# An encoder trunk on one core: where the first modulation products run, how the squares of y are added, and where the last SSD group's items stand

## The chip, the cores and the metric

One core of a Trainium2 chip runs the whole program in one launch. The metric is device microseconds of one execution, given as the median of several runs. Engines are named as the profile names them: PE is TensorE's matmul and PEld its weight load, DVE is VectorE, ACT is ScalarE, POOL is GpSimd and SP is SyncE, which here only issues DMAs.

## The reference, cut to what matters

```python
cond = jax.nn.silu(c)                                  # c: (1, 1024)
for i in range(2):
    mod = cond @ mod_w[i] + mod_b[i]                   # (1, 3072)
    shift, scale, gate = jnp.split(mod, 3, axis=-1)
    hn = rms_norm(x, norm_w[i]) * (1.0 + scale[:, None, :]) + shift[:, None, :]
    y = dilated_attention_mixer(hn, ...) if i == 0 else bi_ssd_mixer(hn, ...)
    x = x + gate[:, None, :] * y                       # x: (1, 1024, 1024)
return rms_norm(x, final_norm_w)

def bi_ssd_mixer(h, ...):                              # its end
    y = y_f + y_b + xs * d_skip[:, None]               # 8 groups of 256 channels
    y = y.reshape(b, s, 2048) * jax.nn.silu(z)
    return rms_norm(y, norm_w) @ w_out
```

## The kernel before, in words

All tensors are held with channels on the 128 partitions and the 1024 tokens along the free axis, so x is eight tiles of 128x1024. The order of work is written out by hand: every engine runs its own instructions in the order in which the program emits them, and waits only for data and for buffers. A dense float32 product is made of three passes, high by high, high by low and low by high, of operands split in two parts: ACT writes the high part (L271 for weights, L293 for the normalised input), DVE the low part (L272, L294). The three matmuls are L376 to L378, and L1004 to L1006 in the output projections. The tile `big` (128x1024) has 27 buffers, and the weight staging tile `wraw` has 4.

**The start (`layer0`).** SP issues the eight tiles of x, then the weights of the modulation in blocks of 128x1024 (`mod_load`, L158). Block 2j is the shift and block 2j+1 the scale of channel tile j; a block holds eight 128x128 pieces, one for each tile of c, and its result is a column of 128 numbers. ACT squares x (L851), PE sums the squares over the partitions with a matrix of ones (L856), and from the sums comes the reciprocal root r: ACT gives a first value (L898, L901), and one Newton step on DVE (L913, L914) mends it, for both halves of the tokens. For a block, `mods` multiplies the weights by the numbers of cond: on POOL (L173, one instruction over the whole block, then two additions, L177) or on ACT (L169, eight instructions). For the blocks that ACT multiplied, and for block 0 and 1, `half` adds the pieces up on DVE (L867, two additions). `fin(j)` lets PE sum what is left over the partitions, two matmuls of one column to a block (L197), and DVE adds the bias (L201) and makes the factor gs (L204). Then `prep(j)` normalises tile j in two halves: DVE L287, ACT L293 (high), DVE L294 (low). The loop over kt (eight turns) runs 18 matmuls of 512 columns to a turn; in it stand `fin(kt + 1)`, `prep(kt + 1)`, the split of the weights of turn kt + 2, the products of blocks 2kt+6 (ACT) and 2kt+7 (POOL), and one `half`. The tables of the rotary angles are made on the side: 44 small instructions on DVE before the loop, the last 14 on POOL, emitted in turn 5.

**The end of layer 1 (`out1`, `first`).** The last SSD group, group 7, runs beside the end of its own dense products and beside the first 14 steps of the output projection; a step is one kt with four matmul groups, 12 matmuls. `weave` spreads the group's items (from `ssd_items`) over this main list by one weight each; `balance`, used for the groups before it, spreads by two estimates of an item, its time on PE and on DVE. The items are A1 (transposes), A2 (the chunk states: L1424 and L1425, then L1434 and L1435), B1 (L1449 and L1455 on DVE, exponentials on ACT), M (L1471, L1473, L1476 on DVE) and B2 (the output matmuls L1487, then L1491 on DVE and a product with z on POOL, L1495). One empty item stands ahead of B1(7). For the projection, `fetch` loads a half tile of y, and `prep(r, kt)` makes its squares (L1554 on POOL for kt under 3, L1556 on ACT), lets POOL add them to a sum (L1558), and splits y times the norm weight: ACT L1561, DVE L1562. The low part is put off to the start of the next step, where DVE runs it in order. Steps use the split y of kt, and `prep` runs up to three steps ahead. The root mean square of y is needed only after the projection (`total`, one matmul with ones).

Of the kernel before, what the change touches and what calls it, by code (L numbers as in the profile page):

```python
# [15 lines left out]
OP = mybir.AluOpType  # L16
# [75 lines left out]
class Trunk:  # L92
# [96 lines left out]

    def mod_fin(self, i, b, *accs):  # L190

        nc = self.nc
        p = self.bank("a2", [P, H2])
        for k, acc in enumerate(accs):
            n = acc.shape[1]
            for c in range(0, n, P):
                nc.tensor.matmul(p[:, k * P:k * P + 1], acc[:, c:c + P], self.ones[:, :1], start=c == 0, stop=c + P == n)  # L197
        m = self.modv[i]
        for k in range(len(accs)):
            c = slice(b + k, b + k + 1)  # L200
            nc.vector.tensor_add(m[:, c], p[:, k * P:k * P + 1], self.vec[:, 16 + 24 * i + b + k:17 + 24 * i + b + k])  # L201
            if b + k < 16 and (b + k) % 2:
                d = (b + k) // 2
                nc.vector.scalar_tensor_tensor(self.gs[i][:, d:d + 1], m[:, c], 1.0,  # L204
                                               self.vec[:, 64 + 8 * i + d:65 + 8 * i + d], op0=OP.add, op1=OP.mult)
# [607 lines left out]
    def layer0(self):  # L813
# [33 lines left out]
        self.w_dma(3)  # L847

# [19 lines left out]

        def fin(j):
            self.mod_fin(0, 2 * j, *[mw.pop(2 * j + s)[:, :2 * P] for s in range(2)])  # L870
# [28 lines left out]
        for h in range(2):  # L899
# [3 lines left out]
            half(h)  # L903
        self.w_split(0)
        mods(2, nc.scalar)
        mods(3, nc.gpsimd)
        def prep(kt):
            if kt < KT:
                for h in range(2):
                    self.hn_tile(0, kt, h * H2, H2, xt[kt][:, h * H2:h * H2 + H2], r[h], self.hn)  # L910
# [4 lines left out]
        fin(0)  # L915
        prep(0)
        self.w_split(1)
        mods(4, nc.scalar)
        mods(5, nc.gpsimd)
        self.finish()  # L920
        self.flush()
        half(2)
        half(4)
        accs = [[self.acc() for _ in range(2)] for _ in range(2)] + [[self.bank("a0", [P, H2], 2) for _ in range(2)]]
        evac = self.evac0 = self.attn_evac(0)
        for kt in range(KT):
            load(kt + 4)
            if 3 < kt + 4 < KT:
                self.w_dma(kt + 4)
            if kt + 3 < KT:  # L930
                mods(2 * kt + 6, nc.scalar)
                mods(2 * kt + 7, nc.gpsimd)
            for m in range(3):
# [6 lines left out]
                elif m == kt == 0:  # L940
                    fin(1)
# [856 lines left out]
```

## Time and profile before

| | us |
|---|---|
| median of 3 runs (1858.36 to 1860.43) | 1859.21 |
| the profiled execution | 1857.47 |
| its span, first to last instruction | 1855.5 |
| PE busy in the span | 1777.3 |
| DVE busy in the span | 1420.6 |
| ACT busy in the span | 956.6 |
| POOL busy in the span | 328.0 |

The page gives busy time and share of each engine, then the span in 40 equal slices with a digit for the busy tenths. A timeline row is start, duration, engine, line, operation, what it writes and reads with shapes, and in brackets the idle time before it and what ended it; a row marked x8 merges eight instructions. PE is busy nearly everywhere, so what can be gained lies where it is not: the first 90 us, and the stretch around the end of the last SSD group, from about 1595 to 1697 us.

### The profile page before, as it was taken

To read this page: it belongs to the slowest core of one execution; us is meant where nothing else is said; L and a number is where in the kernel's file an instruction comes from. 1 tells how busy PE (TensorE), PEld (TensorE's weight loads), DVE (VectorE), ACT (ScalarE), POOL (GpSimd) and SP (SyncE) were. 2 spreads that over 40 slices of the span, in tenths; PEclk is the share of its full clock that TensorE was granted. 3 is DMA by queue.
4 is the path that set the end of the run, shared out by engine and by line. 5 is a ranking of instruction groups with operands and counts; after the bars stand their busy time and mean duration, and the time that the engine had idled before them with its cause. 6 is when DMAs were issued, how large, how long until landed. Compare 5 with 4: busy or idle time off the path is not lost.

```text
span 1855.5 us, 28487 instructions
## 1 busy us (share of the span) xinstructions
PE 1777.3 (96%) x10050; PEld 1453.4 (78%) x10050; DVE 1420.6 (77%) x3219; ACT 956.6 (52%) x2095; POOL 328.0 (18%) x493
## 2 busy tenths in 40 slices
PE   5899999999999999999999999999999999798997
PEld 2678788878788888788878788888888878676787
DVE  7966578766755655666687989899898989897975
ACT  5454445544444544544435656565656565565632
POOL 4611112112211221010110101010101010233310
PEclk7899999999999999999999999999999999999998
DMA  6242234322412131173313243433323342344542
GB/s 249 94 122 90 84 103 129 99 84 87 120 47 58 56 80 55 59 229 136 100 41 97 69 118 82 114 89 93 100 83 108 80 111 78 114 133 140 187 160 96
DMA packets 99733, 193.65 MB, mean 104 GB/s; under 512 B 15624, under 2 KB 23048, under 8 KB 99592
## 3 DMA queue, kind: packets, MB, share of 16 engines
q1 hardware_dynamic: 86600, 167.32, 29.7%
q0 software_dynamic: 12288, 23.86, 4.7%
q8 instruction: 79, 1.29, 0.3%
q10 hardware_dynamic: 704, 0.66, 0.1%
q14 instruction: 62, 0.51, 0.1%
HBM read 169.00 MB, written 16.48 MB: 100 GB/s over the span
## 4 chain that ended last, share of the span: by engine, by line
PE 72%; DVE 17%; ACT 4%; issue 3%; DMA 3%; SPq 0%; ACTq 0%; DVEq 0%; POOL 0%
PE acc L376 16%; PE acc L378 15%; PE acc L377 15%; PE a L1487 3%; PE a L1425 2%; DVE wlo L272 2%; PE a L719 2%; PE a L1004 2%; PE a L1005 2%; PE a L1006 2%; DVE big L1336 2%; PE a L704 2%; PE acc L1006 2%; PE acc L1004 2%; PE acc L1005 2%
## 5 line engine op out<-in xcount | busy, mean ns | idle before, releaser
L376 PE MATMUL acc<-big,whi 128*128 128x512 f32 (+1 forms) x1520 | 631.2, 415 | 13.0 <-ACT big L293 12.4
L377 PE MATMUL acc<-big,whi 128*128 128x512 f32 (+1 forms) x1520 | 595.3, 392 | 2.7 <-DVE big L294 2.6
L378 PE MATMUL acc<-big,wlo 128*128 128x512 f32 (+1 forms) x1520 | 595.3, 392 | 0.3 <-DVE wlo L272 0.3
L376 PEld LDWEIGHTS acc<-big,whi 128*128 128x128 f32 x1520 | 288.0, 189 | 78.6 <-issue 15.8
L378 PEld LDWEIGHTS acc<-big,wlo 128*128 128x128 f32 x1520 | 287.5, 189 | 64.3 <-DVE wlo L272 1.2
L377 PEld LDWEIGHTS acc<-big,whi 128*128 128x128 f32 x1520 | 288.7, 190 | 53.0 <-DVE big L294 6.1
L272 DVE TENSOR_TENSOR wlo<-wraw,whi 128x512 fp32r<-128x512 f32 (+1 forms) x297 | 214.1, 726 | 83.1 <-ACT whi L271 80.1
L271 ACT CAST whi<-wraw 128x512 fp32r<-128x512 f32 (+1 forms) x302 | 181.3, 612 | 85.5 <-PE a L1005 27.3
L695 ACT ACTIVATE sm<-sm,nb 128x256 f32<-128x256 f32 (+1 forms) x192 | 89.3, 466 | 194.9 <-DVE nb L693 192.2
L1336 DVE SCALAR_TENSOR_TENSOR big<-acc,cv,big 128x512 f32<-128x512 f32 (+1 forms) x248 | 169.2, 741 | 6.5 <-ACT big L1328 6.5
L1495 POOL TENSOR_TENSOR big<-big,yt 128x128 f32<-128x128 f32 x128 | 65.3, 531 | 586.7 <-DVE yt L1491 586.6
L1457 ACT ACTIVATE E<-E,nacb 128x128 f32<-128x128 f32 x256 | 81.8, 391 | 143.1 <-DVE E L1449 129.4
L706 DVE COPY pt<-a 128x512 f32<-128x512 f32 (+1 forms) x96 | 57.6, 600 | 73.2 <-PE a L704 73.1
L690 DVE CUSTOM_DVE_ANT_0 sm<-a,cst 128x256 f32<-128x256 f32 (+1 forms) x192 | 64.9, 375 | 60.3 <-PE a L685 60.0
L1004 PE MATMUL a<-big,whi 128*128 128x256 f32 (+1 forms) x304 | 99.2, 326 | 0.0
L1006 PE MATMUL a<-big,wlo 128*128 128x256 f32 (+1 forms) x304 | 98.2, 323 | 0.1
L1005 PE MATMUL a<-big,whi 128*128 128x256 f32 (+1 forms) x304 | 97.9, 322 | 0.0
L1005 PE MATMUL acc<-big,whi 128*128 128x512 f32 x224 | 88.9, 397 | 5.9 <-DVE big L1562 3.1
L592 POOL DMA_DIRECT2D rt<-kT x92 | 50.3, 561 | 243.0 <-ACT kT L532 145.8
L1006 PE MATMUL acc<-big,wlo 128*128 128x512 f32 x224 | 89.5, 399 | 3.2 <-DVE wlo L272 2.4
L1004 PE MATMUL acc<-big,whi 128*128 128x512 f32 x224 | 90.5, 404 | 0.0
L1328 ACT ACTIVATE big<-acc,cv 128x512 f32<-128x512 f32 x62 | 44.5, 770 | 86.4 <-PE acc L378 76.0
(254 smaller groups left out, 3181.7 us busy)
## 6 DMA issues: line engine op xcount, KB each, us to landing
wraw<-in_win SPq DMA_DIRECT2D x186, 256.0 KB
acs<-acsd SPq DMA_DIRECT2D x64, 512.0 KB
wraw<-in_wout SPq DMA_DIRECT2D x112, 256.0 KB
big<-in_modw SPq DMA_DIRECT2D x48, 512.0 KB
yd<-big POOLq DMA_DIRECT2D x14, 512.0 KB, 4.4
big<-yd SPq DMA_DIRECT2D x28, 256.0 KB
vT<-mix POOLq DMA_DIRECT2D x20, 256.0 KB, 4.2
big<-in_xT SPq DMA_DIRECT2D x8, 512.0 KB
```

The lines of the kernel that those rows point to most:

```text
L271: self.nc.scalar.copy(dst_hi, src)
L272: self.late.append((lambda: self.lo_engine.tensor_sub(dst_lo, src, dst_hi.bitcast(F32)), tile))
L376: mm(o, hi[:, cols], x_[:, t0:t0 + n], start=first, stop=False, **kw)
L377: mm(o, hi[:, cols], x_[:, H2 + t0:H2 + t0 + n], start=False, stop=False, **kw)
L378: mm(o, lo[:, cols], x_[:, t0:t0 + n], start=False, stop=last, **kw)
L695: nc.scalar.activation(sm[:, h, :W], sm[:, h, :W], AF.Exp, bias=nb[:, h:h + 1], scale=0.125, accum_out=stat[:, h, 1, i:i + 1])
L1004: mm(o, hi[:, c], x[:, t:t + n], start=kt == 0 and (n == H2 or m % 2 == 0), stop=False, **kw)
L1005: mm(o, hi[:, c], x[:, H2 + t:H2 + t + n], start=False, stop=False, **kw)
L1006: mm(o, lo[:, c], x[:, t:t + n], start=False, stop=kt == nkt - 1, **kw)
L1336: nc.vector.scalar_tensor_tensor(y[:, lo:hi], a[:, lo + o:hi + o], w[:, cv, k:k + 1], y[:, lo:hi], op0=OP.mult, op1=OP.add)
L1457: nc.scalar.activation(E[:, h], E[:, h], AF.Exp, bias=self.nacb[:, c, 4 * g + h:4 * g + h + 1])
L1495: nc.gpsimd.tensor_mul(z, z, t[:, r])
```

## The change

In the start, the products of blocks 1, 2, 3, 4, 6, 10 and 14 are made by PE itself: eight matmuls of one column on the raw weights, with a column of cond as the moving operand. Block 0 is multiplied by DVE, the other eight (5, 7, 8, 9, 11, 12, 13, 15) by ACT, and these nine go through `half`. POOL multiplies none. Weight blocks 8 to 11 are asked for ahead of the first wait of SP, and 12 to 15 in the first two turns. The Newton step runs for the first half of the tokens, then `fin(0)` and `prep` of that half, and then for the second. `fin(1)` is put ahead of the loop.

In `out1`, for the first half of the tokens, y is fetched in pairs of tiles, its squares are all made by ACT and written in pairs into a tile of their own; POOL adds seven such tiles into the first, three of them inside the 14 steps and four behind them, and PE sums both halves of the tile (two matmuls for one). `balance` takes the place of `weave`, the empty item has 6.0 us of DVE time to its name, and the fetches of the first y tiles stand some items ahead of their `prep`.

```diff
-    def mod_fin(self, i, b, *accs):
...
         self.w_dma(3)
+        load(4)
+        load(5)
...
+        pe, act = (1, 2, 3, 4, 6, 10, 14), (5, 7, 8, 9, 11, 12, 13, 15)
+
         def fin(j):
-            self.mod_fin(0, 2 * j, *[mw.pop(2 * j + s)[:, :2 * P] for s in range(2)])
+            p = self.bank("a0", [P, 2, P], 2) if j < 2 else self.bank("a2" if j % 2 else "a3", [P, 2, P])
+            for k in (1, 0):
+                w = mw.pop(2 * j + k)
+                n = KT if 2 * j + k in pe else 2
+                for c in range(n):
+                    x = self.cond[:, c:c + 1] if n == KT else self.ones[:, :1]
+                    nc.tensor.matmul(p[:, k, :1], w[:, c * P:c * P + P], x, start=c == 0, stop=c == n - 1)
+            m = self.modv[0]
+            c = slice(2 * j, 2 * j + 2)
+            nc.vector.tensor_add(m[:, c], p[:, :, 0], self.vec[:, 16 + 2 * j:18 + 2 * j])
+            nc.vector.scalar_tensor_tensor(self.gs[0][:, j:j + 1], m[:, 2 * j + 1:2 * j + 2], 1.0,
+                                           self.vec[:, 64 + j:65 + j], op0=OP.add, op1=OP.mult)
...
-        mods(0, nc.gpsimd, 1)
-        mods(1, nc.gpsimd, 1)
         for h in range(2):
             merge(6, slice(h * H2, h * H2 + H2))
             total(sq[6], False, True, (h,))
+        mods(0, nc.vector, 1)
+        half(0)
...
             nc.scalar.activation(u[h], r[h], AF.Square)
-            half(h)
         self.w_split(0)
-        mods(2, nc.scalar)
-        mods(3, nc.gpsimd)
...
             nc.vector.scalar_tensor_tensor(r[h], u[h], 1.5, r[h], op0=OP.add, op1=OP.mult)
-        fin(0)
-        prep(0)
+            if h == 0:
+                fin(0)
+            prep(0, (h,))
         self.w_split(1)
-        mods(4, nc.scalar)
-        mods(5, nc.gpsimd)
+        mods(5, nc.scalar)
         self.finish()
         self.flush()
-        half(2)
-        half(4)
+        fin(1)
...
         for kt in range(KT):
-            load(kt + 4)
+            if kt < 2:
+                load(kt + 6)
...
-            if kt + 3 < KT:
-                mods(2 * kt + 6, nc.scalar)
-                mods(2 * kt + 7, nc.gpsimd)
...
             self.w_split(kt + 2)
+            for b in (2 * kt + 6, 2 * kt + 7):
+                if b in act:
+                    mods(b, nc.scalar)
             self.finish()
             self.flush()
-            if kt + 3 < KT:
-                half(2 * kt + 6)
+            for b in (2 * kt + 4, 2 * kt + 5):
+                if b in act:
+                    half(b)
...
         if g == 7:
-            items.append((1500, lambda: None, 0, 0))
+            items.append((1500, lambda: None, 0, 6.0))
...
+        def add_pair(k):
+            for n in range(2):
+                c = slice(n * H2, n * H2 + H2)
+                nc.gpsimd.tensor_add(pairs[0][:, c], pairs[0][:, c], pairs[k][:, c])
+            pairs[k] = None
...
-            if r == 0 and kt < 3:
-                nc.gpsimd.tensor_mul(sq, y, y)
-            else:
-                nc.scalar.activation(sq, y, AF.Square)
-            if kt:
+            if r == 0:
+                if kt % 2 == 0:
+                    pairs.append(self.big())
+                    if kt in (8, 10, 12):
+                        add_pair(kt // 2 - 3)
+                sq = pairs[-1][:, kt % 2 * H2:kt % 2 * H2 + H2]
...
+            nc.scalar.activation(sq, y, AF.Square)
+            if kt and r:
                 nc.gpsimd.tensor_add(ys[r]["sq"][:, :H2], ys[r]["sq"][:, :H2], sq)
...
         def first(ps):
             m = tail[0][:]
-            for i in range(4):
-                m.insert(len(m) - 10 + 2 * i, (1, lambda i=i: prep(0, i)))
-            weave(m + [(2600, f) for _, f in ps[0][:14]], tail[1])
+            for at, f, k in ((1, prep, 3), (2, prep, 2), (3, fetch, 4), (4, prep, 1), (6, prep, 0), (8, fetch, 2), (12, fetch, 0)):
+                m.insert(len(m) - at, (1, lambda f=f, k=k: f(0, k), 0, 0.7 if f is prep else 0))
+            balance(m + [(2600, f, 2.76, 1.4) for _, f in ps[0][:14]], tail[1])
+            add_pair(4)
+            add_pair(5)
...
                 prep(0, kt)
+            add_pair(6)
...
+            add_pair(7)
```

## Rows read from the trace of the kernel before

**Rows 1.** The page: busy time, share of the span, instructions.

```profile
PE 1777.3 (96%) x10050; PEld 1453.4 (78%) x10050; DVE 1420.6 (77%) x3219; ACT 956.6 (52%) x2095; POOL 328.0 (18%) x493
```

**Rows 2.** Stretches of the start: window and length, busy of each engine, granted clock, DMA.

```profile
7.30:20.30 13.00, 12.93 (x24) 5.42 (x24) 9.20 (x36) 9.27 (x10) 3.26 (x2) 1.00 1.02 411
20.30:37.30 17.00, 1.97 (x8) 1.85 (x8) 16.71 (x15) 6.45 (x16) 15.24 (x10) 0.56 0.41 158
37.30:93.50 56.20, 49.80 (x200) 38.48 (x201) 50.67 (x74) 30.75 (x76) 30.61 (x27) 0.83 0.34 118
```

**Rows 3.** Timeline of PE, 37 to 94 us.

```profile
39.28 0.79 PE L378 MATMUL acc<-big,wlo 128*128 128x512 f32 x1 [0.34 <-DVE wlo L272]
...
41.16 1.70 PE L197 MATMUL a<-ones,big 128*128 128x1 f32 x8
...
58.27 0.80 PE L377 MATMUL acc<-big,whi 128*128 128x512 f32 x1 [1.72 <-DVE big L294]
...
69.88 0.94 PE L197 MATMUL a<-ones,big 128*128 128x1 f32 x8
...
89.48 0.39 PE L376 MATMUL acc<-big,whi 128*128 128x512 f32 x1
...
93.33 0.39 PE L378 MATMUL a<-big,wlo 128*128 128x512 f32 x1
```

**Rows 4.** Timeline of DVE, 20 to 90 us.

```profile
20.85 3.29 DVE L867 TENSOR_TENSOR big<-big 128x512 f32<-128x512 f32 x2
...
26.61 2.38 DVE L913 SCALAR_TENSOR_TENSOR big<-big,sm 128x512 f32<-128x512 f32 x1
...
65.67 1.14 DVE L867 TENSOR_TENSOR big<-big 128x512 f32<-128x512 f32 x2
...
74.66 1.82 DVE L867 TENSOR_TENSOR big<-big 128x512 f32<-128x512 f32 x2
...
86.94 1.41 DVE L287 SCALAR_TENSOR_TENSOR kT<-big,gs,pt 128x512 f32<-128x512 f32 x2
88.48 1.41 DVE L294 SCALAR_TENSOR_TENSOR big<-kT,modv,big 128x512 fp32r<-128x512 f32 x2
```

**Rows 5.** Timeline of POOL: the first products, first and last of the angle tables.

```profile
17.04 6.82 POOL L173 TENSOR_TENSOR big<-big,cond 128x1024 f32<-128x1024 f32 x3 [16.08 <-DMA big<-in_modw]
...
71.28 2.04 POOL L481 TENSOR_TENSOR vT<-vT,vT 128x192 f32<-128x192 f32 x2
...
83.15 0.83 POOL L498 TENSOR_TENSOR V<-vT,vT 128x192 f32<-128x192 f32 x1
```

**Rows 6.** ACT's groups, 20 to 93.5 us: count, busy, mean ns, idle before.

```profile
L169 ACT ACTIVATE big<-big,cond 128x128 f32<-128x128 f32 x56 | 17.0, 388 | 0.0
```

**Rows 7.** Stretches of the late part, columns as in Rows 2.

```profile
1595.40:1628.80 33.40, 28.27 (x128) 21.94 (x126) 24.54 (x45) 12.55 (x31) 9.78 (x10) 0.95 0.47 134
1628.80:1641.50 12.70, 12.70 (x71) 10.48 (x69) 9.16 (x18) 11.16 (x26) 3.53 (x2) 1.00 0.49 160
1641.50:1696.50 55.00, 44.30 (x291) 32.94 (x290) 54.76 (x106) 37.03 (x86) 22.99 (x22) 0.97 0.44 126
```

**Rows 8.** DVE's groups, 1595.4 to 1628.8 us, columns as in Rows 6.

```profile
L1562 DVE SCALAR_TENSOR_TENSOR big<-big,sv,big 128x512 fp32r<-128x512 f32 x4 | 3.1, 776 | 7.4 <-ACT big L1561 7.4
...
L272 DVE TENSOR_TENSOR wlo<-wraw,whi 128x512 fp32r<-128x512 f32 x4 | 2.7, 684 | 0.7 <-ACT whi L271 0.7
```

**Rows 9.** Timeline of DVE at the first projection steps.

```profile
1631.92 0.42 DVE L1455 TENSOR_TENSOR cb<-a,cst 128x256 f32<-128x256 f32 x1 [2.99 <-PE a L1452]
...
1644.35 1.76 DVE L1562 SCALAR_TENSOR_TENSOR big<-big,sv,big 128x512 fp32r<-128x512 f32 x1
```

**Rows 10.** DVE's groups, 1628.8 to 1697.5 us.

```profile
L1562 DVE SCALAR_TENSOR_TENSOR big<-big,sv,big 128x512 fp32r<-128x512 f32 x10 | 11.2, 1115 | 0.0
```

**Rows 11.** POOL's groups, 1628.8 to 1697.5 us.

```profile
L1558 POOL TENSOR_TENSOR big<-big,big 128x512 f32<-128x512 f32 x10 | 16.6, 1659 | 41.0 <-ACT big L1556 41.0
L1495 POOL TENSOR_TENSOR big<-big,yt 128x128 f32<-128x128 f32 x15 | 11.3, 773 | 11.7 <-DVE yt L1491 11.6
```

More of the change, by code (lines that the diff above doesn't have):

```diff
@@ L188, in mod_acc @@
             nc.vector.tensor_add(out, acc, odd)
-    def mod_fin(self, i, b, *accs):
[L192 to L205, printed above, removed]
     def mod_sum(self, i, b, accs):
@@ L902, in layer0, with prep @@
             nc.scalar.activation(u[h], r[h], AF.Square)
-            half(h)
         self.w_split(0)
-        mods(2, nc.scalar)
-        mods(3, nc.gpsimd)
-        def prep(kt):
+        def prep(kt, hs=range(2)):
             if kt < KT:
-                for h in range(2):
+                for h in hs:
                     self.hn_tile(0, kt, h * H2, H2, xt[kt][:, h * H2:h * H2 + H2], r[h], self.hn)
@@ L1530, in out1 @@
         nc, io = self.nc, self.io
-        xin, x2, cut, ybuf = {}, {}, {}, {}
+        xin, x2, cut, ybuf, pairs = {}, {}, {}, {}, []
         ys, st = [{} for _ in range(2)], [{} for _ in range(2)]
@@ L1536, in fetch @@
                 return
-            buf = ybuf[r, kt] = self.big()
-            if kt < 14:
-                nc.sync.dma_start(buf[:, :H2], self.yd[kt][:, H2 * r:H2 * r + H2])
+            if r:
+                buf = self.big()
+                ybuf[r, kt] = buf, buf[:, :H2]
+                if kt < 14:
+                    nc.sync.dma_start(buf[:, :H2], self.yd[kt][:, H2:])
+            elif kt < 14:
+                buf = self.big()
+                for k in range(2):
+                    y = buf[:, H2 * k:H2 * k + H2]
+                    ybuf[r, kt - kt % 2 + k] = buf, y
+                    nc.sync.dma_start(y, self.yd[kt - kt % 2 + k][:, :H2])
+            else:
+                ybuf[r, kt] = None, None
+        def add_pair(k):
[3 more added lines that the diff above has]
+            pairs[k] = None
         def prep(r, kt):
@@ L1545, in prep @@
             fetch(r, kt)
[L1546 to L1547 removed]
+            buf, y = ybuf.pop((r, kt))
             if kt >= 14:
                 y = self.ylast[kt - 14][:, H2 * r:H2 * r + H2]
[L1550 removed]
+            if r == 0:
[4 more added lines that the diff above has]
+                sq = pairs[-1][:, kt % 2 * H2:kt % 2 * H2 + H2]
+            elif kt == 0:
                 ys[r]["sq"] = self.big()
                 sq = ys[r]["sq"][:, :H2]
[L1553 to L1557 removed]
+            else:
+                sq = buf[:, H2:]
+            nc.scalar.activation(sq, y, AF.Square)
+            if kt and r:
                 nc.gpsimd.tensor_add(ys[r]["sq"][:, :H2], ys[r]["sq"][:, :H2], sq)
@@ L1615, in total @@
             def total():
-                ys[r]["s"] = self.all_sum(ys[r], 0, H2, self.acc())
+                if r:
+                    ys[r]["s"] = self.all_sum(ys[r], 0, H2, self.acc())
+                    return
+                p = ys[r]["s"] = self.acc()
+                for n in range(2):
+                    nc.tensor.matmul(p, self.ones, pairs[0][:, n * H2:n * H2 + H2], start=n == 0, stop=n == 1)
             def start():
                 ys[r]["v"] = self.rstd_start(ys[r]["s"], 2 * D, H2)
-            return [(0.5, out), (1, total), (1, start)]
+            return [(0.5, out)] + [(2, lambda: None)] * (r == 0) + [(1, total), (1, start)]
         def first(ps):
             m = tail[0][:]
-            for i in range(4):
-                m.insert(len(m) - 10 + 2 * i, (1, lambda i=i: prep(0, i)))
-            weave(m + [(2600, f) for _, f in ps[0][:14]], tail[1])
+            for at, f, k in ((1, prep, 3), (2, prep, 2), (3, fetch, 4), (4, prep, 1), (6, prep, 0), (8, fetch, 2), (12, fetch, 0)):
[3 more added lines that the diff above has]
+            add_pair(5)
             for _, f in ps[1][:2]:
```

5 lines of the change are left out of this document (removed).

## The prediction

> **What bounds the kernel now.** I read the page first: PE is busy 96% of the span [rows 1], so a change can give back only what PE loses, some 78 us, and the question is where it loses it. The windows tell: most of it lies at the two places that the diff touches. At the start, PE ends the sums of squares at 20.3, and until 37.3 it is busy for 1.97 us of 17, while DVE is busy for 16.71 of 17 and POOL for 15.24 [rows 2]. The first matmul that needs a low part of the weights runs at 39.28, and the last of the eight turns is issued at 93.33 [rows 3]. In the loop DVE is busy for 50.67 of 56.2 us, POOL for 30.61, and the mean granted clock of PE is 0.83 [rows 2]: PE waits for DVE, and falls to 1.2 GHz after waits, such as the 1.72 us ahead of 58.27 [rows 3].
>
> The DVE timeline says why DVE takes so long. The two additions of one `half` take 1.14 us at 65.67, but 3.29 at 20.85, where POOL runs its 128x1024 products of 2.3 us each; one 512-wide step of Newton takes 2.38 [rows 4, 5], while other two-operand instructions of that width take 0.70 (half of 1.41) [rows 4]. DVE is slowed by POOL's work beside it.
>
> The late windows show a second place. From 1595.4 to 1628.8 PE is idle for 5.1 of 33.4 us [rows 7]; in it DVE stands 7.4 us at L1562, the low part of y, waiting for ACT, which itself waited for y to be loaded [rows 8]. From 1641.5 to 1696.5 DVE is busy for 54.76 of 55 us and PE for 44.30 [rows 7]: DVE is the bound. There too it is slowed: L1562 means 1115 ns where POOL adds squares, against 776 before [rows 8, 10].
>
> **The change part by part: up to the first matmul.** I work out the quiet time of what DVE does from 20.3 to 37.3. Two scalings of the sums (0.7 each), two `half` (1.14 each), four Newton steps and two L287 (0.70 each), and the small additions with gs (0.4) come to 8.3 us, so 8.4 of the 16.7 are POOL's doing. The change takes POOL's products out; one `half` goes (block 1 is PE's), and the other, with a product of 1.2 us for block 0, goes into the time before 20.3, where DVE is busy for only 9.20 of 13 us [rows 2]; block 0 arrived by 17.04 [rows 5], so some 0.4 us of it may stick out past 20.3, which I take into the range. That leaves 16.7 - 8.4 - 2.3 = 6.0 us.
>
> But one thing comes with it. The last 14 instructions of the angle tables stand on POOL behind all products, from 71.28 to 83.98, 12.7 us [rows 5]. Nothing is ahead of them now, and what they read is done on DVE before 17 us, so they run from about 17 to 30, under this very chain. Their price is read where they ran before: a `half` beside them took 1.82 against 1.14 at 74.66 [rows 4], the worst of the pairs there; I take a third on the mean, 2.0 us, with nothing and a doubling (6.0) as ends. The doubling is what POOL's large products did. The chain then takes 8.0 to 8.4 instead of 17.0: **8.6 us earlier** (4.6 to 10.6), the first full matmul group near 30.7. The weights are there: blocks 0 to 7 come by the same queue as before, 8 to 11 behind them, where the DMAs stood idle (0.41 of the stretch used [rows 2]). `fin(1)` stands ahead of the loop in PE's queue, 16 matmuls; 4 take 0.94 us [rows 3], so 3.8, or 6.8 at the low clock (1.70 for 4 [rows 3]). PE is free from 20.3 and does ten for `fin(0)` first, so it ends by 30, in time.
>
> **The loop.** It took 93.7 - 39.3 = 54.4 us. After the change the turns hang on one ring: `fin` on PE, then DVE's addition and gs (0.3), L287 (1.41), L294 (1.41), the low part of the weights (0.5, three quarters of the 0.68 of 512 columns [rows 8]), then the `half`s of the blocks that ACT multiplied, and these are what the next `fin` waits for. That is 3.6 us of DVE for each of six turns and seven `half`s at 1.14, 29.6 in all. ACT keeps up: a block costs it 8 x 0.3 = 2.4 us [rows 6], in the worst turn two, beside 1.9 of its own work. `fin` is dearer on PE: 10 matmuls (2.4 us) where one block is raw, 4 (0.95) for blocks 8, 9 and 12, 13; six of them cost 4 x 2.4 + 2 x 0.95 = 11.5. With some 6.5 us for the first turn, which starts at the low clock, and 4.1 for the last (89.48 to 93.33, and one issue [rows 3]): 6.5 + 29.6 + 11.5 + 4.1 = 51.7. PE's own work in a turn, 4.1 + 2.4, is under the ring's 7.3, so the ring sets it, and PE waits 0.6 to 1.6 us in each turn. I add 1.7 us for falls of the clock after such waits, since it fell after 1.72 at 58.27: 53.4, **1.0 us gained** (2.7 to minus 8). So the ring takes back most of what the quiet DVE gives: the added PE work is not hidden, as it stands between two DVE stages of the same turn.
>
> **The last SSD group.** The items' order I worked out from their weights. In the dense part the A items come about one dense step earlier, the first y tiles are fetched seven items before the end and split only two items before it, so DVE no longer stands at L1562 for a load. PE's 5.1 us idle there should go: **5 us** (1 to 6.5; some falls to A2's own chain). Then `balance` puts B1(7) behind the third projection step instead of the first: two steps of 12 matmuls at 0.227 us, 5.4 us later on PE, which cancels the 5. So the first L1455 of DVE, at 1631.92, which waits for that matmul [rows 9], comes at about the same time, and from there DVE is the bound. What it has left is less: the low parts for two more steps are behind it (0.74 + 0.68 each, 2.8 us), and of the additions of squares on POOL six instead of ten [rows 11] fall into this stretch. Each costs DVE about a microsecond: L1562 took 1.76 at 1644.35 [rows 9], 0.98 over the quiet 776 [rows 8], so 4.0. Products with z on POOL stay. Against it, at the end the last two chunks stand together behind the last step, and DVE waits for ACT's exponentials: 1.5 us, bounded by 0 and 4 (no row shows this order). Net 2.8 + 4.0 - 1.5 = 5.3. The second matmul of `total` is a plain float32 one of 512 columns; 24 instructions made 12 of these in 12.93 us [rows 2], so 1.1 us more, in a part where PE is the bound. The eight additions that POOL makes behind the steps fall where DVE has room, and cost nothing; without this room, up to 8 us of DVE. **4.2 us gained** (9 to minus 2).
>
> **The sum.** 8.6 + 1.0 + 4.2 = 13.8 us. The profiled execution took 1857.47, so 1843.7 on its scale; the median of the runs is 1.7 above it, and from 1859.21 comes **1845.4 us**.
>
> **Rivals.** (1) The angle tables on POOL hold DVE as much as its products did: the chain doubles, 4.0 us of the gain go, 1849.4. For: each of their instructions reads SBUF. Against: 1.82 and not 3.29 for a `half` [rows 4]. The Trainium skill's page SBUF - State Buffer, section "Who interferes with whom", says that a DVE instruction with two SBUF inputs is blocked for the whole of a GpSimd instruction that reads SBUF, if that came first; by it the tables can cost DVE at most their own length, and the 1.82 agrees.
>
> (2) The late part gives nothing: the chunks that come later, and the wait at the end, take all of it. 1859.2 - 9.6 = 1849.6. For: DVE has no idle time there [rows 7], so order alone can't help. Against: six additions for ten.
>
> (3) Both parts give their upper ends: 10.6 + 2.7 + 7.5, 1838.4. For: both upper ends need only quiet on DVE.
>
> (4) Runs of one-column matmuls let the clock fall. In the four turns with ten, `fin` takes 4.25 instead of 2.35 (by 1.70 against 0.94 [rows 3]), and about a third of the wide matmuls' time is lost, 3 us a turn, 12 in all: 1857.4, no difference. For: the turns with waits show 0.83. Against: at 69.88 four of them run at 0.94, at full clock.
>
> (5) Slower: PE stays at 1.2 GHz through the whole loop, since a turn now has 2.4 us of one-column work and a wait in it. All its work takes 1.8 times as long (1.70 over 0.94): eight turns of 4.1 and 11.5 of `fin` make 80 us instead of 53.4. From 30.7 the loop ends at 110.7, 17 later than before, 12.8 later with the late part's gain: 1872. It decides once PE's work in a turn, 1.8 x 6.5 = 11.7, is over the ring's 7.3 in most turns. Against: before, the clock came back within each turn (0.83 as a mean).
>
> **How the numbers follow.** Forecast 0.45, (1) 0.13, (2) 0.12, (3) 0.13, (4) 0.12, (5) 0.05. A change under 0.2%, 3.7 us, is about what a measurement can't tell from none; the border is 1855.5. Faster: the forecast, (1), (2), (3) and a third of (4), 0.87; same: the rest of (4), 0.08; slower 0.05. The range goes from (3) with 1.4 of the unknown costs below it, 1837, to just short of (4), 1856.
>
> **What would show it.** First L378 of the loop near 30 to 31 and the last near 84; no L173 on POOL, and the angle tables on it at 17 to 30; PE's waits in the loop ended by L867 or gs, not by L293. Late: DVE's wait at L1562 gone, L1455 of B1(7) near 1631.9 less the 9.6 gained ahead of it, six L1558-like additions in the steps, B2(0) some 5 us earlier than the start's gain alone would put it. Wrong if the loop's clock lies under 0.75, if the first L378 comes after 35, or if DVE's busy share in the steps stays at 0.99 for as long as 65 us.

## The result and the profile after

The changed kernel takes **1840.92 us** (median; 1839.99 to 1841.28), the kernel before 1859.82 beside it: a ratio of 0.9896 (95% interval 0.9878 to 0.9913), 18.9 us faster. Beside the experiments below the kernel before had medians of 1856.76 to 1857.84, so a fair figure is 16 to 19 us. Its profiled execution has a span of 1839.0 us against 1855.5, 16.5 less, and it is these 16.5 that the traces can place. Lines of the changed kernel differ in number: mm3's three matmuls, before L376 to L378, are L359 to L361; `fin`'s matmuls are L866, `half` is L852, Newton L912 and L913, `prep` L270, L276, L277, the low parts of weights L255; late, the pair additions are L1554, the low part of y L1582, B1 L1450, M L1469, B2 L1485, the steps L1002 to L1004.

| place | before, us | after, us | gained so far | here |
|---|---|---|---|---|
| first full group of the loop (first matmul on a low part) | 39.28 | 29.87 | 9.4 | +9.4 |
| PE leaves the loop (first matmul behind its last turn) | 93.56 | 86.49 | 7.1 | -2.3 |
| fourth of ACT's table loads behind 70 us | 158.24 | 147.16 | 11.1 | +4.0 |
| an ACT table load as the dense part with the last group begins | 1591.61 | 1581.29 | 10.3 | -0.8 |
| first projection step | 1628.78 | 1613.26 | 15.5 | +5.2 |
| last B2 ends | 1696.8 | 1677.5 | 19.3 | +3.8 |
| end of the span | 1855.5 | 1839.0 | 16.5 | -2.8 |

The windows of after, to be laid beside [rows 2] and [rows 7]: busy time of each engine with its number of instructions, granted clock of PE, DMA share, GB/s.

```profile
core 0: us, PE busy (x) PEld busy (x) DVE busy (x) ACT busy (x) POOL busy (x), PEclk, DMA share, GB/s
7.30:20.30 13.00, 13.00 (x27) 5.71 (x27) 11.93 (x39) 9.05 (x10) 4.16 (x3) 1.00 1.02 408
20.30:30.00 9.70, 9.70 (x54) 9.34 (x54) 9.00 (x15) 6.58 (x14) 8.96 (x12) 0.61 1.03 404
29.87:86.49 56.62, 52.17 (x240) 42.97 (x239) 34.18 (x66) 33.25 (x85) 2.06 (x3) 0.85 0.28 99
1578.60:1612.00 33.40, 31.51 (x167) 25.01 (x163) 28.18 (x56) 20.29 (x45) 6.75 (x10) 0.95 0.39 137
1612.00:1624.70 12.70, 12.70 (x59) 10.50 (x58) 7.73 (x18) 10.52 (x22) 0.00 (x0) 1.00 0.37 120
1624.70:1679.70 55.00, 44.91 (x316) 36.58 (x315) 53.76 (x115) 39.13 (x92) 14.46 (x21) 0.95 0.51 139
1677.50:1683.50 6.00, 6.00 (x21) 4.79 (x20) 5.86 (x7) 3.00 (x5) 5.47 (x6) 0.72 0.28 87
```

Three things are to be seen. The chain ahead of the loop is over at 30 instead of 39. In the loop DVE is no longer full (34.18 of 56.62 us, where it was 50.67 of 56.2 [rows 2]), and yet PE's clock is 0.85, hardly above the 0.83 it was. In the steps DVE is as full as before, but the stretch is 3.8 us shorter.

**The start.** DVE's and PE's rows of the timeline (start, duration, instruction, how many; in brackets how long it stood idle and for whom), and the first and the last of POOL's:

```profile
22.21 0.69 DVE L912 SCALAR_TENSOR_TENSOR big<-big,sm 128x512 f32<-128x512 f32 x1 [0.49 <-ACT big L903]
22.93 0.97 DVE L913 SCALAR_TENSOR_TENSOR pt<-big,pt 128x512 f32<-128x512 f32 x1
28.95 1.17 DVE L255 TENSOR_TENSOR wlo<-wraw,whi 128x384 fp32r<-128x384 f32 x2
...
16.14 4.04 POOL L464 TENSOR_TENSOR vT<-vT,vT 128x192 f32<-128x192 f32 x2 [15.18 <-DVE vT L461]
29.68 0.90 POOL L481 TENSOR_TENSOR V<-vT,vT 128x192 f32<-128x192 f32 x1
...
20.11 1.84 PE L866 MATMUL a<-cond,big 128*128 128x1 f32 x16
22.26 6.75 PE L866 MATMUL a<-cond,big 128*128 128x1 f32 x32
28.87 0.77 PE L359 MATMUL acc<-big,whi 128*128 128x512 f32 x1
29.87 0.64 PE L361 MATMUL acc<-big,wlo 128*128 128x512 f32 x1
```

A Newton step takes 0.69 to 0.97 us, not up to 2.38 [rows 4]; the angle tables run on POOL under the whole chain, 16.14 to 30.58, and DVE feels them little (e5 gives the price). PE's run of one-column matmuls for `fin(1)` is different: 16 instructions at 20.11 take 1.84 us, the 32 from 22.26 on 6.75, nearly twice as long each, in a stretch where PE has no gap at all. The granted clock is 0.61 on the mean from 20.3 to 30, so most of it is at the lower of the two levels, 1.2 of 2.4 GHz.

**The loop.** PE's rows of `fin`, and the last two turns:

```profile
42.65 0.58 PE L866 MATMUL a<-ones,big 128*128 128x1 f32 x4 [0.84 <-issue]
43.09 1.93 PE L866 MATMUL a<-cond,big 128*128 128x1 f32 x16
51.26 1.02 PE L866 MATMUL a<-ones,big 128*128 128x1 f32 x8 [2.01 <-DVE big L852]
72.74 0.58 PE L866 MATMUL a<-ones,big 128*128 128x1 f32 x4 [1.00 <-DVE big L852]
73.18 3.09 PE L866 MATMUL a<-cond,big 128*128 128x1 f32 x16
76.13 0.77 PE L359 MATMUL acc<-big,whi 128*128 128x512 f32 x1
82.40 0.40 PE L359 MATMUL acc<-big,whi 128*128 128x512 f32 x1
86.49 0.39 PE L359 MATMUL acc<-big,whi 128*128 128x512 f32 x1
```

PE waits in front of `fin` for the `half` that DVE has just added, as the ring wants it (at 42.65, too, where the row names no engine: that `half` ends at 42.56), and the last `fin` runs at the low clock (3.09 us for what took 1.93 at 43.09), and so does the group behind it (76.13 to 82.40, 6.3 us; the last group, at full clock, takes 4.1).

**The last SSD group.** POOL's pair additions and the DVE instructions that run beside them, with one that runs alone:

```profile
1603.36 3.05 POOL L1554 TENSOR_TENSOR big<-big,big 128x512 f32<-128x512 f32 x2 [12.99 <-ACT big L1576]
1637.01 3.04 POOL L1554 TENSOR_TENSOR big<-big,big 128x512 f32<-128x512 f32 x2
1646.45 2.65 POOL L1554 TENSOR_TENSOR big<-big,big 128x512 f32<-128x512 f32 x2
1679.36 13.19 POOL L1554 TENSOR_TENSOR big<-big,big 128x512 f32<-128x512 f32 x8
...
1629.73 1.14 DVE L1469 SCALAR_TENSOR_TENSOR W<-cb,dt,W 128x128 f32<-128x128 f32 x4
1637.52 3.21 DVE L1469 SCALAR_TENSOR_TENSOR W<-cb,dt,W 128x128 f32<-128x128 f32 x4
1645.75 3.49 DVE L1469 SCALAR_TENSOR_TENSOR W<-cb,dt,W 128x128 f32<-128x128 f32 x4
```

Four additions are left in the DVE-bound steps instead of ten, since the first pair is added already at 1603.36, in the dense part; the two pairs in the steps stretch M's four instructions from 1.14 to 3.21 and 3.49 us. DVE's 7.4 us of standing at the low part of y [rows 8] are gone.

### The profile page after: what moved, and what is told of

Its sections match the earlier page's. It is cut to its first block, busy times and chain, and to the rows that moved or that the text cites. A ratio compares the mean times of both kernels' runs of the same rounds, so it can differ in the third digit from the quotient of the medians.

```text
span 1839.0 us, 28627 instructions
## 1 busy us (share of the span) xinstructions
PE 1781.9 (97%) x10136; PEld 1465.9 (80%) x10136; DVE 1393.7 (76%) x3212; ACT 960.7 (52%) x2106; POOL 284.0 (15%) x466
## 4 chain that ended last, share of the span: by engine, by line
PE 41%; DVE 11%; ACT 3%; issue 2%; DMA 0%; DVEq 0%; POOL 0%; ACTq 0%; POOLq 0%
PE acc L359 8%; PE acc L361 7%; PE acc L360 7%; PE a L1485 3%; PE a L1423 2%; DVE big L1334 2%; PE a L1004 2%; PE a L1002 2%; PE a L1003 2%; DVE W L1469 2%; PE acc L1004 2%; PE acc L1003 2%; PE acc L1002 1%; DVE wlo L255 1%; DVE acs L1474 1%
## 5 line engine op out<-in xcount | busy, mean ns | idle before, releaser
L359 PE MATMUL acc<-big,whi 128*128 128x512 f32 (+1 forms) x1520 | 630.4, 415 | 0.7 <-DVE big L1334 0.7
L361 PE MATMUL acc<-big,wlo 128*128 128x512 f32 (+1 forms) x1520 | 594.7, 391 | 0.0
L359 PEld LDWEIGHTS acc<-big,whi 128*128 128x128 f32 x1520 | 288.2, 190 | 65.9 <-issue 15.6
L361 PEld LDWEIGHTS acc<-big,wlo 128*128 128x128 f32 x1520 | 287.1, 189 | 63.8 <-DVE wlo L255 0.4
L255 DVE TENSOR_TENSOR wlo<-wraw,whi 128x512 fp32r<-128x512 f32 (+1 forms) x297 | 210.6, 714 | 87.7 <-ACT whi L254 84.1
L1493 POOL TENSOR_TENSOR big<-big,yt 128x128 f32<-128x128 f32 x128 | 61.6, 502 | 633.8 <-DVE yt L1489 633.8
L673 DVE CUSTOM_DVE_ANT_0 sm<-a,cst 128x256 f32<-128x256 f32 (+1 forms) x192 | 64.9, 375 | 57.7 <-PE a L668 57.5
L1004 PE MATMUL a<-big,wlo 128*128 128x256 f32 (+1 forms) x304 | 98.8, 325 | 1.8 <-DVE wlo L255 1.8
L1002 PE MATMUL a<-big,whi 128*128 128x256 f32 (+1 forms) x304 | 99.8, 328 | 0.0
L1469 DVE SCALAR_TENSOR_TENSOR W<-cb,dt,W 128x128 f32<-128x128 f32 x256 | 86.6, 395 | 6.9 <-ACT W L1457 5.0
L1002 PE MATMUL acc<-big,whi 128*128 128x512 f32 x224 | 89.4, 399 | 0.0
```

The costliest lines, as they stand in the source:

```text
L255: self.late.append((lambda: self.lo_engine.tensor_sub(dst_lo, src, dst_hi.bitcast(F32)), tile))
L359: mm(o, hi[:, cols], x_[:, t0:t0 + n], start=first, stop=False, **kw)
L361: mm(o, lo[:, cols], x_[:, t0:t0 + n], start=False, stop=last, **kw)
L1002: mm(o, hi[:, c], x[:, t:t + n], start=kt == 0 and (n == H2 or m % 2 == 0), stop=False, **kw)
L1004: mm(o, lo[:, c], x[:, t:t + n], start=False, stop=kt == nkt - 1, **kw)
L1469: nc.vector.scalar_tensor_tensor(W[:, h], cb[:, 1], self.dt[:, c, hh:hh + 1], W[:, h], op0=OP.mult, op1=OP.add)
```

## The experiments

Each is given with its ratio to the kernel before, measured beside it on the same chip. As that kernel's median differs between these measurements by up to 3.1 us (1856.76 to 1859.82), two rows are compared by their own medians and spans, and not by their ratios.

| kernel | median, us | ratio (95% interval) | span, us |
|---|---|---|---|
| after | 1840.92 | 0.9896 (0.9878 to 0.9913) | 1839.0 |
| e1_start: before + the start alone | 1849.22 | 0.9951 (0.9935 to 0.9968) | 1846.1 |
| e2_late: before + the late part alone | 1851.22 | 0.9955 (0.9940 to 0.9970) | 1850.0 |
| e3_pairs: before + the pairs alone | 1853.81 | 0.9977 (0.9967 to 0.9987) | 1852.9 |
| e4_balance: before + the placing alone | 1854.67 | 0.9978 (0.9967 to 0.9988) | 1854.0 |
| e5_tables: after, tables on DVE | 1840.18 | 0.9908 (0.9892 to 0.9925) | 1839.5 |
| e6_raw_first: after, raw block first | 1840.65 | 0.9909 (0.9881 to 0.9938) | 1838.5 |
| e7_all_act: after, no raw blocks in the loop | 1839.88 | 0.9907 (0.9893 to 0.9922) | 1838.1 |
| e8_sin_late: after, sine held back | 1844.33 | 0.9933 (0.9913 to 0.9953) | 1841.4 |
| e9_no_gap: after, empty item without weight | 1840.25 | 0.9906 (0.9892 to 0.9921) | 1839.0 |
| e10_ahead: after, halves a turn earlier | 1832.08 | 0.9865 (0.9848 to 0.9881) | 1830.5 |

A bound on what a span can tell: four profiles with the start of before have the first matmul on a low part at 38.92, 39.28, 40.30 and 40.73. A difference of one microsecond between two spans says nothing.

### Taking the change apart: e1, e2

e1_start has all edits of the diff down to the loop, e2_late all of the last group and the squares.

> The kernel before with the start of the change alone; the end of layer 1 is as before. Theory (the parts don't touch each other): the first L378 of the loop near 30, PE at the first attention unit some 11 us earlier than before, as in the changed kernel, and a little of that lost up to the last SSD group: 10 us faster than before, 9 to 11.5. Rival (the start only shows its gain because the late part has room for it): under 8.

> The kernel before with the late part of the change alone. Theory: 5 us in the dense part, 4 in the projection steps, 1 to 3 given back behind them: 6 to 8 us faster than before, and with the start alone the two add up to the changed kernel's time within 1 us. Rival (the two overlap): the sum is off by more than 2 us.

The spans are 9.4 and 5.5 shorter, 14.9 together against 16.5, and the ratios multiply to 0.9906 against 0.9896: the parts add up, as far as it can be measured, though not within the 1 us that the theory asked for. By span e1 lies in its expected 9 to 11.5 us and e2 just under its 6 to 8; by the medians they are 8.6 and 6.6 us faster. e1 also tells what the first group waits for. In it the run of one-column matmuls for `fin(1)` is faster (4.36 us for the same 32 instructions, 6.75 in after), and the group still comes no earlier, since it then waits for DVE. PE's rows of e1:

```profile
28.93 0.80 PE L360 MATMUL acc<-big,whi 128*128 128x512 f32 x1 [1.74 <-DVE big L277]
30.35 0.80 PE L361 MATMUL acc<-big,wlo 128*128 128x512 f32 x1 [0.62 <-DVE wlo L255]
```

So DVE's chain and PE's slow run end together, and a quicker PE alone gives nothing.

### Taking the late part apart: e3, e4

e3_pairs has the pairs, but the old order of items; from e2_late to it:

```diff
-            items.append((1500, lambda: None, 0, 6.0))
+            items.append((1500, lambda: None, 0, 0))
...
-            for at, f, k in ((1, prep, 3), (2, prep, 2), (3, fetch, 4), (4, prep, 1), (6, prep, 0), (8, fetch, 2), (12, fetch, 0)):
-                m.insert(len(m) - at, (1, lambda f=f, k=k: f(0, k), 0, 0.7 if f is prep else 0))
-            balance(m + [(2600, f, 2.76, 1.4) for _, f in ps[0][:14]], tail[1])
+            for i in range(4):
+                m.insert(len(m) - 10 + 2 * i, (1, lambda i=i: prep(0, i)))
+            weave(m + [(2600, f) for _, f in ps[0][:14]], tail[1])
```

e4_balance has the order, the early fetches and the empty item, but the old squares, one addition on POOL to each; from before to it:

```diff
-            items.append((1500, lambda: None, 0, 0))
+            items.append((1500, lambda: None, 0, 6.0))
...
-            for i in range(4):
-                m.insert(len(m) - 10 + 2 * i, (1, lambda i=i: prep(0, i)))
-            weave(m + [(2600, f) for _, f in ps[0][:14]], tail[1])
+            for at, f, k in ((1, prep, 3), (2, prep, 2), (3, fetch, 5), (3, fetch, 4), (4, prep, 1), (6, prep, 0),
+                             (8, fetch, 3), (8, fetch, 2), (12, fetch, 1), (12, fetch, 0)):
+                m.insert(len(m) - at, (1, lambda f=f, k=k: f(0, k), 0, 0.7 if f is prep else 0))
+            balance(m + [(2600, f, 2.76, 1.4) for _, f in ps[0][:14]], tail[1])
```

> The kernel before with the pairs alone: y fetched in pairs, squares on ACT, pair additions on POOL; the order of the last group's items and the places of the first splits stay as they were. Theory (DVE is held by POOL's additions in the steps, so fewer of them is the gain there; the wait for loads in the dense part stays): 3 to 5 us faster than before, nearly all between the first projection step and the last B2. Rival (order is what gains): under 2 us.

> The kernel before with the placing by load alone: balance, the empty item of 6.0, and early fetches of the first six tiles ahead of their splits; squares and their additions stay as they were, one by one. Theory: the 5 us in the dense part come, and in the steps DVE loses what it gains: 4 to 6 us faster than before, with the time from the first step to the last B2 at 65 us or more (67.9 before, 64.2 in the changed kernel). Rival (the order is good only with the squares in pairs): under 3 us.

| | first step begins | last B2 ends | steps to there | from there to the end |
|---|---|---|---|---|
| before | 1628.78 | 1696.8 | 68.0 | 158.7 |
| e3_pairs | 1628.35 | 1692.5 | 64.1 | 160.4 |
| e4_balance | 1624.75 | 1693.4 | 68.7 | 160.6 |
| e2_late | 1622.97 | 1688.2 | 65.2 | 161.8 |
| after | 1613.26 | 1677.5 | 64.2 | 161.5 |

Here the two causes part. The pairs shorten the steps by 3.9 us and leave the dense part nearly alone (the first step begins 0.4 us earlier), where DVE still stands 7.7 us at the low part of y. The placing takes 4.0 us from the dense part and nothing from the steps. Both then give back about 2 us behind the last B2. By the medians e3 is 4.0 us faster than before, inside its 3 to 5, and e4 3.2, under its 4 to 6. DVE's groups in that dense part (line, instruction, tiles, shapes, count, busy us, mean ns, idle us ahead of it and for whom), first of e3, then of e4:

```profile
L1584 DVE SCALAR_TENSOR_TENSOR big<-big,sv,big 128x512 fp32r<-128x512 f32 x4 | 3.0, 749 | 7.7 <-ACT big L1583 7.7
```

```profile
L1562 DVE SCALAR_TENSOR_TENSOR big<-big,sv,big 128x512 fp32r<-128x512 f32 x2 | 3.5, 1776 | 0.0
```

The 1776 ns of e4 beside the 749 of e3 are the old additions on POOL again, 1.0 us to one instruction.

### Where the pieces stand on PE: e9

```diff
-            items.append((1500, lambda: None, 0, 6.0))
+            items.append((1500, lambda: None, 0, 0))
```

> The kernel after with the weight of the empty item ahead of the last group's B items set from 6.0 to 0, so that B1(7) and all that follows it stand about two projection steps earlier on PE. The forecast's working held that these two steps, 5.4 us, cancel what the dense part gives. If so, the last B2 ends up to 5 us earlier and the span is 3 to 5 us shorter than the 1839.0 of after. Rival: the first B1 then waits for DVE and ACT, which still make the low parts and the exponentials for it, and PE stands where it did, so the last B2 moves by less than 1 us, or the waits only change place: span 1838 to 1841.

The rival was right. B1(7)'s matmul comes 5.6 us earlier (1615.8 for 1621.4), the last B2 ends at 1678.1 for 1677.5, and the span is the same 1839.0. The windows of e9 over the last two stretches of after show why:

```profile
1612.00:1624.70 12.70, 12.70 (x59) 10.50 (x58) 10.97 (x25) 12.02 (x28) 0.00 (x0) 1.00 0.43 142
1624.70:1679.70 55.00, 45.72 (x312) 36.65 (x311) 50.82 (x108) 36.92 (x86) 13.83 (x20) 0.92 0.47 135
```

DVE does 10.97 + 50.82 = 61.8 us of work there, and in after 7.73 + 53.76 = 61.5: the same work with the idle time elsewhere.

### POOL's tables: e5

```diff
             if kt == 5:
-                self.rope_engine = nc.gpsimd
                 turn(99)
```

> The changed kernel with the last 14 instructions of the angle tables on DVE, in turn 5 of the loop, where DVE waits for PE, in place of POOL, where they run from 16 to 30 us. Theory (they hold DVE in the start as L913 at 0.97 and L277 at 0.81 show, about 1.5 us in all, but the first wide matmul waits for the 32 one-column matmuls of fin(1) until 28.87 anyhow): low parts ready 1 to 1.5 us earlier, first wide matmul unchanged, whole time within 1 us of the changed kernel. Rival (DVE's chain sets the start): 1.5 us faster or more. Third: 14 more instructions on DVE in turn 5 delay the loop, 2 us slower.

1839.5 for 1839.0, as expected, but not because the tables cost DVE nothing. With POOL idle from 20 to 30, the chain from the first L912 to the end of the second L255 takes 7.06 us on DVE (22.49 to 29.55), and 7.91 in after (22.21 to 30.12): 0.85 us. The `half` ahead of that chain takes 1.15 us here and 1.70 in after. None of it shows, since PE's run for `fin(1)` (22.54 to 29.20 here) then ends last, and the first low part is met at 30.06, for 29.87 in after. With e1 this makes two bounds that lie within a microsecond; no run here took both away.

### What sets the loop: e6, e7, e10

e6 lets `fin` begin with the raw block, which needs no `half`; e7 gives the raw blocks 4, 6, 10 and 14 to ACT; e10 leaves every block where it is, but has the halves added one turn earlier, so that no `fin` waits for a half that DVE has only just added; for that, ACT makes the products of three blocks earlier, too. The edits, in this order:

```diff
-            for k in (1, 0):
+            for k in ((0, 1) if 2 <= j and 2 * j in pe else (1, 0)):
```

```diff
-        pe, act = (1, 2, 3, 4, 6, 10, 14), (5, 7, 8, 9, 11, 12, 13, 15)
+        pe, act = (1, 2, 3), (4, 5, 6, 7, 8, 9, 10, 11, 12, 13, 14, 15)
+        mods(4, nc.scalar)
         mods(5, nc.scalar)
```

```diff
+            for b in {1: (8,), 2: (11,), 3: (13,)}.get(kt, ()):
+                mods(b, nc.scalar)
             for m in range(3):
                 if m == 0 < kt < KT - 1:
                     fin(kt + 1)
...
-            for b in (2 * kt + 6, 2 * kt + 7):
-                if b in act:
-                    mods(b, nc.scalar)
+            for b in {0: (7,), 1: (9,), 2: (12,), 3: (15,)}.get(kt, ()):
+                mods(b, nc.scalar)
...
-            for b in (2 * kt + 4, 2 * kt + 5):
-                if b in act:
-                    half(b)
+            for b in {0: (5, 7), 1: (8, 9), 2: (11,), 3: (12, 13), 4: (15,)}.get(kt, ()):
+                half(b)
```

> The changed kernel with the order of the two blocks turned round in fin(2), fin(3), fin(5) and fin(7): the raw block, whose eight matmuls wait for nothing on DVE, ahead of the one that waits for half. Theory (the ring through DVE and PE sets the turns): the eight matmuls of 1.9 us hide in PE's wait, and the loop ends earlier by PE's waits of these turns, 0.2 + 0.8 + 0 + 1.0, about 2 us, and more if the clock falls less often. Rival (PE's own work and its low clock set the loop): under 1 us.

> The changed kernel with blocks 4, 6, 10 and 14 multiplied by ACT too and added by half, so that only blocks 1, 2 and 3 are raw and no turn has a run of 16 one-column instructions on a raw block. PE's work falls by 4 x 1.45 = 5.8 us, DVE's rises by 4 x 1.14. Theory (the raw blocks cost more on PE, in line, than the halves on DVE, and the clock falls in turns that have them): turns of 6.9 us in place of 7.4 to 8.6, the loop 3 to 5 us shorter, the whole 2 to 5 us faster than the changed kernel. Rival (DVE sets the turns, or ACT with 6.8 us a turn): same or slower.

> The kernel after with the halves that ACT has multiplied added one turn earlier in the loop (ACT starts the products 8, 11 and 13 ahead of the shifts of its turn, so that they are there), no work left out. Theory that the loop hangs on the ring of fin, DVE's chain and the halves for the next fin: fin no longer waits for a half of its own turn, PE's own 6.5 us set the turn in place of 7.3 to 8.5, and the loop, 56.6 us from its first full group to its last turn's end in after, takes 50 to 53; span 1833 to 1837. Rival, that the granted clock is the bound (0.69 to 0.84 in the loop, runs of one-column matmuls in four of the turns): the loop stays over 55 us with a lower clock and fewer waits, span 1838 to 1841.

By their medians e6 and e7 both take as long as after, which the rival of each had and the theory of neither. In e6 PE leaves the loop at 84.62 for 86.49, about the 2 us expected; but ACT's fourth table load is only 1.1 us earlier (146.04), no more than after and e9, which are the same up to there, differ (147.16 and 148.33), and the span 0.5. Its four runs lie further apart than those of any other kernel here, 1832.50 to 1845.97 us, and the shortest has the highest mean granted clock, 0.993 where the others have 0.986 to 0.988: how the clock falls may be worth as much as an edit. In e7 a `fin` is 1.4 us shorter where it had a raw block, but there a second half of 1.15 us stands in front of it, and the turns from `fin` to `fin` take 7.2 to 8.3 us (starts at 37.95, 46.10, 53.28, 60.62, 67.88, 76.17): the ring is as long as it was. Its first `fin` in the loop even comes 2.7 us later than in after (37.95 for 35.22), for DVE stands 1.94 us waiting for ACT, which has block 4's product to make first. That wait and one of PE's, of e7:

```profile
33.84 1.41 DVE L277 SCALAR_TENSOR_TENSOR big<-kT,modv,big 128x512 fp32r<-128x512 f32 x2 [1.94 <-ACT big L276]
53.28 1.02 PE L866 MATMUL a<-ones,big 128*128 128x1 f32 x8 [2.00 <-DVE big L852]
```

e10 cuts the ring and leaves the work of every engine as it is, and the span falls by 8.5 us to 1830.5. It has the lowest median of all: 1832.08 us (1831.52 to 1833.59), where e9, measured beside it, has 1840.25 (1838.92 to 1840.74). Its windows and PE's rows of `fin`:

```profile
50.00:60.00 10.00, 10.00 (x49) 8.42 (x48) 8.15 (x16) 7.54 (x21) 0.00 (x0) 0.83 0.08 29
29.94:76.55 46.61, 46.42 (x240) 39.42 (x240) 33.98 (x66) 32.75 (x85) 1.35 (x2) 0.94 0.32 115
...
41.67 0.50 PE L866 MATMUL a<-ones,big 128*128 128x1 f32 x4
42.03 1.93 PE L866 MATMUL a<-cond,big 128*128 128x1 f32 x16
48.05 0.95 PE L866 MATMUL a<-ones,big 128*128 128x1 f32 x8
53.08 0.50 PE L866 MATMUL a<-ones,big 128*128 128x1 f32 x4
53.44 1.93 PE L866 MATMUL a<-cond,big 128*128 128x1 f32 x16
```

There are no brackets: PE waits for nobody. The turns take 6.4 and 5.0 us, PE's own work, but for one of 8.0, from 53.08, in which the clock falls; and the loop runs from 29.94 to 76.55, 46.6 us for 56.6. That is shorter than the 50 to 53 expected, which went by 6.5 us for a turn. The two windows of the loop tell what the 10 us are: PE stands idle for 0.2 us instead of 4.5, which is 4.3, and its mean clock of 0.94 for 0.85 loses 2.8 us instead of 8.5, which is 5.7. Both changed together; how much of the 5.7 comes from the missing waits, and how much from chance, no run separates. DVE does as much as before the cut (33.98 and 34.18 us).

### Behind the loop: e8

```diff
-            if kt == 6:
-                self.rope_out(cs)
...
+                    if m == 0:
+                        nc.scalar.copy(self.eps2, accs[0][0][:, :1])
+                        self.rope_out(cs)
                     evac[m](*accs[m])
```

> The changed kernel with the sine of the angle tables held back by some 4 us, until the first matmul group of the last turn has ended, so that it stands to PE as in the kernel before (3 us ahead of the next dense block, in place of 7). Theory (the 4 us that the changed kernel gains between the loop and 158 us come from the tables and the rotation starting earlier against PE): PE's wait for the first attention scores returns, 2 us or more, and the second table switch of the first unit comes 3 to 5 us later; whole time 3 to 5 us longer than the changed kernel. Rival (that gain comes from elsewhere, the DVE being free): under 1 us.

The span is 2.4 us longer, under the 3 to 5 expected and over the rival's 1; by the medians e8 is 3.7 to 4.5 us longer than e5 to e7, measured beside it. ACT's table loads of after, then of e8, and PE's wait at the first attention scores in each:

```profile
79.45 1.28 ACT L486 ACT_TABLE_LOAD   x1
147.16 1.28 ACT L532 ACT_TABLE_LOAD   x1
115.04 0.39 PE L667 MATMUL a<-K,Q 128*128 128x256 f32 x1 [0.23 <-DVE stat L673]
```

```profile
83.82 1.28 ACT L487 ACT_TABLE_LOAD   x1
149.85 1.28 ACT L533 ACT_TABLE_LOAD   x1
117.71 0.39 PE L668 MATMUL a<-K,Q 128*128 128x256 f32 x1 [1.47 <-DVE stat L674]
```

The same wait took 2.43 us before. From PE's leaving of the loop to ACT's fourth table load it is 64.7 us before, 60.7 in after, 63.0 in e8, but 61.5 in e9, which has the start of after. So 1.5 to 2.3 of the 4.0 us that after gains behind the loop are there because ACT is done with the loop earlier than PE is, and can switch its table and make the angles' sine while PE still works. What the rest is, and why 0.8 of it is lost again by 1591 (1.9 in e1), stays open.

## Why the prediction was right, step by step

The forecast was 13.8 us less, 1845.4; measured were 18.9 less, inside the range of 1837 to 1856 and with the sign that had 0.87. By places the span's 16.5 are 9.4 from the start, 2.3 lost in the loop, 3.2 behind it, and 6.2 from the late part, where 8.6, 1.0, nothing and 4.2 were forecast. That the sum came near is in part luck: the loop's error of 3.3 us was made up by a gain of 3.2 behind it that the forecast didn't have.

**Start chain: 8.6 forecast, 9.4 measured.** Removing POOL's products gave DVE's quiet durations, and block 0's `half` on DVE stuck out of the squares' stretch by some 0.2 us (it ends at 20.46). The term taken too high was the price of the tables on POOL, 2.0 us; e5 puts it at 0.85 in DVE's chain (and 0.55 in the `half` ahead of it), so rival (1), with 6.0, has no ground. That `fin(1)` at the low clock ends by 30 was right (28.9), with nothing to spare.

**Loop: 1.0 gained forecast, 2.3 lost.** The ring was the right mechanism, which e6, e7 and e10 bear out, but its sum of 51.7 + 1.7 us became 56.6. By places: to the first `fin` 5.4 us for 6.5; the five turns to the last `fin` 37.5 for 35.1, because PE and DVE hand over twice in a turn, which the sum left out (about 0.3 us a turn: in the one from 42.65, PE works 2.37 us and DVE 5.95, 45.05 to 51.00, but the turn has 8.61), and because one turn, from 51.26, was PE's, with a group at the low clock (0.7); from the last `fin` to the end 13.75 for 10.1, most of it clock, since `fin` takes 3.4 us where the one at 42.65 took 2.2, and the group behind it 6.3 where the one behind 42.65 took 4.2; most of the rest is that the sum had DVE's 3.6 there and not PE's own 4.2. So the mis-sized term is the clock's, put at 1.7 us: it is 3.2 in the last two turns alone. Rivals (4) and (5) named something real, but (4) asked 12 us of it and (5) 27. e10 adds what the forecast didn't ask: nothing forces the ring. With the halves a turn ahead the loop takes 10 us less, 5.7 of them by the clock.

**Behind the loop: nothing forecast, 4.0 measured.** The forecast took PE's last turn for what the rest hangs on. It hangs in part on ACT's table load, 10.2 us earlier than before (79.45 for 89.64), and e8 gives back 1.5 to 2.3 us when it is held.

**Dense part and the place of B1(7): 5 us forecast and cancelled again, and so it came.** The first projection step gains 5.2 us; e4 shows 4.0 of it with the placing alone. B1(7) then stands two steps later behind it, and its first instruction on DVE that waits for PE starts at 1621.84 for 1631.92 [rows 9], 10.1 us earlier where 10.3 had been gained ahead:

```profile
1621.84 0.42 DVE L1453 TENSOR_TENSOR cb<-a,cst 128x256 f32<-128x256 f32 x1 [1.75 <-PE a L1450]
```

e9 adds what the forecast didn't weigh: the two steps cost nothing in the end. Without them this instruction starts at 1616.19, but from there to the last B2 DVE has 57.5 us of work instead of 54.5, and idles for 4.4 us instead of 1.2.

**From there to the last B2: 5.3 forecast, 9.2 measured.** This is the term that was mis-sized in the late part. The windows from this instruction to the end of the last B2, before and after (columns as in the windows above):

```profile
1631.90:1696.80 64.90, 54.20 (x347) 40.91 (x346) 64.09 (x122) 45.20 (x107) 26.82 (x24) 0.97 0.47 138
1621.83:1677.50 55.67, 45.58 (x323) 37.11 (x322) 54.52 (x118) 40.39 (x96) 12.78 (x18) 0.97 0.52 140
```

DVE's work falls by 9.6 us. Four instructions fewer are left, three low parts of weights and one of y, 2.8 us at their quiet 0.68 and 0.75, as forecast. The other 6.8 are the additions on POOL: six fewer stand beside DVE and not four, at 1.1 us each where the forecast had 1.0. e3 shows this price alone: with the very instructions that before has in this stretch and four additions fewer, DVE's busy time is 59.84 us, 4.25 less. The wait at the end, put at 1.5 us, is 0.3 (DVE idles for 1.15 us in all, 0.81 before).

**Behind the last B2: 1.1 lost forecast, 2.8 measured.** The second `total` matmul costs nearly what was said: the four instructions of L1641 take 1.88 us, two took 1.02 before. Left out was the clock. The step behind the last B2 runs at 0.72 for 6 us, where it was 1.00 before, which loses 0.28 x 6 = 1.7. It is 0.77 in e4, which has no second matmul, and 0.72 in e3, which has the old order, but 1.00 in e1: either half of the late part brings it. Why stays open. PE's last two waits ahead of it are 3.48 and 2.37 us (ahead of 1671.24 and 1676.44), but 1.30 and 2.03 in e3, where the clock falls as well, and 2.04 and 2.50 before, where it doesn't.

Rival (2), that the late part gives nothing, fell with e2 to e4. Rival (3), both upper ends, had 1838.4 and came near in time, but by other places: the loop gave none of its 2.7, and what follows the loop gave 4.0.

## What to carry to other kernels

When an engine is relieved in a loop, look for the ring of hand-overs that remains, and add up a whole round of it, hand-overs included; then ask whether its slowest link can be done one turn earlier, because that costs no work and here was worth about half as much again as the change (8.5 us to 16.5). Where one engine is full over a stretch, moving pieces on the others gains nothing (e9), and what helps is work taken from it, or from an engine that slows it when both run, as POOL's additions slow DVE. Give the granted clock a term of its own, with a range: it was the largest error in the loop and behind the last B2, and e6's runs differ with it.

## What was not expected of the hardware

PE being busy without a gap did not keep its clock at 2.4 GHz: in after the granted clock was 0.61 from 20.3 to 30 with PE busy for 9.70 of 9.70 us, and a one-column instruction took 0.21 us instead of 0.12. In e10, where PE is idle for 0.2 us of the whole loop, the wide matmuls behind the run at 53.44 still fall to 0.63 us each for seven instructions:

```profile
56.59 0.63 PE L361 MATMUL acc<-big,wlo 128*128 128x512 f32 x1
59.15 0.63 PE L361 MATMUL acc<-big,wlo 128*128 128x512 f32 x1
59.90 0.39 PE L360 MATMUL a<-big,whi 128*128 128x512 f32 x1
```

But the same run at 42.03 was followed by a group at full clock, so it doesn't fall each time. Which of the two happens, no run here settles. The Trainium skill (TensorE: Matmul & The Clock Gate, Part 1) ties the clock to how busy PE has been; by busy time as the profile counts it these rows don't agree.
